# Recurrent chunk states of a hybrid encoder block: the scaling by the decay moves from VectorE to ScalarE

## The chip, the cores and the metric

The kernel runs on one core of one Trainium2 chip. The metric is device time in microseconds, the median of several runs. Engines are called as the profile calls them: PE is TensorE's matmuls, DVE is VectorE, ACT is ScalarE, POOL is GpSimd, SP is the engine that issues most DMAs.

## What is computed

One layer of an encoder on x of 1 x 1024 x 1024 in float32: a layer norm; one large projection `h @ w_in`; a dilated sliding-window attention; a bidirectional gated recurrence (HGRN2) of 8 heads with 128 keys and 128 values each; gates and output projections; two more layer norms around a SwiGLU feed-forward part. The change lies in the recurrence, which the reference computes by chunks of 64 tokens (cut):

```
def gla_chunkwise(q, k, v, logf):
    cum = jnp.cumsum(logf.reshape(b, h, n, c, kd), axis=3)
    q_dec = q * jnp.exp(cum)
    ...
    cum_last = cum[..., -1:, :]
    u = jnp.einsum('bhnck,bhncv->bhnkv', k * jnp.exp(cum_last - cum), v)
    decay = jnp.exp(cum_last[..., 0, :])

    def step(state, inp):
        d, uu = inp
        return d[..., None] * state + uu, state
    ...
    o_inter = jnp.einsum('bhnck,bhnkv->bhncv', q_dec, s_start)
```

It is done twice, forward and on the flipped sequence. The state of a chunk is a 128 x 128 matrix per head and direction.

## The kernel before

**The stream of projections.** The first part of the kernel (`phase1`, L1214) is a stream of projection products on PE. Each float32 matrix is split into a high part, cast by ACT (L212), and a low part, a subtraction on POOL (L220); a product is three matmuls (L268, L269, L270). The big products are formed from sums of blocks in the manner of Strassen and Winograd, so that sums of weights (L606 and neighbours) come before the matmuls and evacuations (L484, L509, L510, L633 and others, on DVE and ACT) come after them. Products use four PSUM banks, called pj.

**The side work.** Between the steps of that stream, a generator takes a step of the recurrence or of the attention: heads 0 and 1, a unit of attention, heads 2 and 3, a unit, heads 4 and 5, a unit, heads 6 and 7. This lies between 145 and 1010 us. All of it uses four more PSUM banks, called sd, that rotate (`ps_sd`). The program is written in this order, and the framework's scheduler, which simulates a timeline, moves instructions of each engine; each engine then takes its own queue strictly in order.

**One head** (`hgrn_side`, L1174). Chunks are taken as 8 blocks of 128 tokens, with gates scaled around the middle of each block, so that the decay of a whole block is the product of two factors: `dec[:, 0]` from the middle to the block's end and `dec[:, 1]` from its start to the middle.
- `hgrn_dir` (L1044), once per direction: gates and scans, reciprocals (L1079, L1082), the scaled queries `qd` (L1083, L1084; L1083 is also the last reader of the tile `fa`), and the decays, copied by POOL (L1088, L1089).
- `hgrn_keys` (L1091): PE transposes four blocks of keys into an sd bank (L1097), ACT copies them out to `hkT` (L1098); two banks per direction.
- `hgrn_states` (L1102): PE makes the seven chunk products (L1113) into two sd banks, four and three. DVE runs the chain E: L1122 for the first block, then for each of the other six L1124 (E times `dec[:, 1]` plus the product, read from PSUM) and L1125 (times `dec[:, 0]`). After each block ACT writes E times `dec[:, 1]` into the state tile S, called `hS` (L1116). A state is 13 operations of DVE and 7 of ACT; there are 16 states, 8 heads by 2 directions.
- S is a slot of 1024 columns: that of direction 0 is where `fa` was, that of direction 1 is where the second direction's `fb` was. The chain's tiles `hR` rotate among three.
- `hgrn_scores` (L1129), twice, each for four blocks and with two sd banks: L1138 to L1142. They need no state.
- `hgrn_out` (L1152): the scores times values plus `qd` times S, L1164.

The order within a head is: keys of direction 0, states 0, keys of direction 1, states 1, both halves of the scores, output. Since sd banks rotate, the scores' second pair of banks are those of a states step before it, and a bank can be written again only when its last reader is through.

Of the kernel before, what the change touches and what calls it, by code (L numbers as in the profile page):

```python
# [10 lines left out]
F32 = mybir.dt.float32  # L11
F32R = mybir.dt.float32r
I32 = mybir.dt.int32
AF = mybir.ActivationFunctionType
OP = mybir.AluOpType
# [57 lines left out]


CST_PAD = 32
SMT_PAD = 832
TABW = 128 * 5 + 64 + 256 + 384 + 256 + 192


class Block:  # L80
# [963 lines left out]
    def hgrn_dir(self, h, d, st):  # L1044

        nc = self.nc
        ga, gb, gna = (z[:, d, h:h + 1] for z in (self.ga, self.gb, self.gna))
        t3 = st[f"t{d}"].rearrange("p (c i) -> p c i", i=128)
        q3 = st["q"].rearrange("p (c i) -> p c i", i=128)

        A = st["fa"][:, HALF * d:HALF * d + HALF].rearrange("p (c i) -> p c i", i=64)
        B = self.slot(7 + d, "fb", (8, 66))
        if d == 0:
            nc.gpsimd.memset(A[:, :, 0:1], 0.0)
            nc.gpsimd.memset(B[:, :, 65:66], 0.0)
            nc.scalar.activation(A[:, :, 1:64], t3[:, :, 65:128], AF.Identity, bias=gb, scale=ga)
            nc.scalar.activation(B[:, :, 0:65], t3[:, :, 0:65], AF.Identity, bias=gb, scale=ga)
        else:
            nc.gpsimd.memset(A[:, :, 63:64], 0.0)
            nc.gpsimd.memset(B[:, :, 0:1], 0.0)  # L1060
            nc.scalar.activation(A[:, :, 0:63], t3[:, :, 0:63], AF.Identity, bias=gb, scale=ga)
            nc.scalar.activation(B[:, :, 1:66], t3[:, :, 63:128], AF.Identity, bias=gb, scale=ga)
        nc.gpsimd.tensor_scalar(t3, t3, gna, ga, op0=OP.mult, op1=OP.add)

        def scan(f, n, rev):
            f = f.rearrange("p c i -> p (c i)")
            f = f[:, ::-1] if rev else f
            nc.vector.tensor_tensor_scan(f, f, self.d1[n], 0.0, op0=OP.mult, op1=OP.add)

        scan(A, 64, d == 1)  # L1070
        scan(B, 66, d == 0)
        far = slice(64, 128) if d == 0 else slice(0, 64)
        near = slice(0, 64) if d == 0 else slice(64, 128)
        R = B[:, :, 1:65]
        qd = self.slot(2 + 2 * d, "qd", (8, 128))
        nc.gpsimd.tensor_mul(t3[:, :, near], t3[:, :, near], R)
        yield
        for c in (slice(0, 4), slice(4, 8)):
            nc.vector.reciprocal(qd[:, c, far], A[:, c])  # L1079
        nc.gpsimd.tensor_mul(t3[:, :, far], t3[:, :, far], qd[:, :, far])  # L1080
        for c in (slice(0, 4), slice(4, 8)):
            nc.vector.reciprocal(qd[:, c, near], R[:, c])  # L1082
        nc.vector.scalar_tensor_tensor(qd[:, :, far], q3[:, :, far], CQ, A, op0=OP.mult, op1=OP.mult)  # L1083
        nc.vector.scalar_tensor_tensor(qd[:, :, near], q3[:, :, near], CQ, qd[:, :, near], op0=OP.mult, op1=OP.mult)  # L1084
        st["qd", d], st["ki", d] = qd, t3

        dec = st["dec", d] = self.smt.tile([128, 2, 8], F32, name="dec", tag="dec", bufs=4)
        nc.gpsimd.tensor_copy(dec[:, 0, :], A[:, :, 63 if d == 0 else 0])  # L1088
        nc.gpsimd.tensor_copy(dec[:, 1, :], B[:, :, 0 if d == 0 else 65])  # L1089

    def hgrn_keys(self, st, d):  # L1091

        nc, out = self.nc, []
        for b in (0, 1) if d == 0 else (1, 0):
            pt, kT = self.ps_sd(), self.half3("hkT")
            for k in range(4):
                nc.tensor.transpose(pt[:, 128 * k:128 * (k + 1)], st["ki", d][:, 4 * b + k, :], self.ident)  # L1097
            nc.scalar.copy(kT, pt.rearrange("p (k c) -> p k c", k=4))  # L1098
            out.append(kT)
        return out  # L1100

    def hgrn_states(self, st, d, kT, vT):  # L1102

        nc, dec = self.nc, st["dec", d]
        S = self.slot(6 + d, "hS", (8, 128))
        cs = list(range(8)) if d == 0 else list(range(7, -1, -1))
        E = None
        for b in range(2):
            ps = self.ps_sd().rearrange("p (k c) -> p k c", k=4)
            part = cs[4 * b:4 * b + 4]  # L1110
            for jj, c in enumerate(part):
                if c != cs[-1]:
                    nc.tensor.matmul(ps[:, jj, :], kT[b][:, c % 4, :], vT[:, c, :], start=True, stop=True)  # L1113
            for jj, c in enumerate(part):
                if E is not None:
                    nc.scalar.activation(S[:, c, :], E, AF.Copy, scale=dec[:, 1, c:c + 1])  # L1116
                if c == cs[-1]:
                    continue

                En = self.sm.tile([128, 128], F32, name="hR", tag="hR", bufs=3)  # L1120
                if E is None:
                    nc.vector.tensor_scalar(En, ps[:, jj, :], dec[:, 0, c:c + 1], None, op0=OP.mult)  # L1122
                else:
                    nc.vector.scalar_tensor_tensor(En, E, dec[:, 1, c:c + 1], ps[:, jj, :], op0=OP.mult, op1=OP.add)  # L1124
                    nc.vector.tensor_scalar(En, En, dec[:, 0, c:c + 1], None, op0=OP.mult)  # L1125
                E = En
        return S

    def hgrn_scores(self, st, b):  # L1129
# [84 lines left out]
    def phase1(self):  # L1214
# [9 lines left out]
        self.smt = side.enter_context(self.pool("smt"))  # L1224
        self.pad(self.smt, SMT_PAD)
        self.cst1 = side.enter_context(self.pool("cst1"))
# [623 lines left out]
```

## Time and profile before

| | us |
|---|---|
| median of 3 runs | 2102.98 |
| lowest and highest | 2100.78 and 2104.03 |
| the profiled execution | 2102.44 |
| span of its profile | 2100.6 |
| busy in the span: POOL | 1093.8 |
| the largest group on POOL, L220 from `wa`, 272 times | 377.1 |
| the largest group on ACT, L212 from `wa`, 272 times | 167.6 |

The span is what the profile covers of the execution; the rest lies around it. Rows of a page or a view give the line of the kernel, the engine, the operation, output and inputs, and the shape. A number after `x` is a count. In a timeline a row begins with the start and the duration in us, and brackets hold the idle time before it and what ended it. In a group's row, after the bar, come busy us and the mean ns of one instruction, then the idle time before and what ended it. The granted clock is the share of TensorE's full rate that the throttle allowed in a stretch; its mean in this execution is 0.987. A busy PE at half the clock does half the work.

### The profile page before, as it was taken

The page shows a single profiled execution, that of the slowest core. Times are in us where ns is not written, and L with a number is a line of the kernel's source. Part 1 is how long each engine was busy: PE and PEld are TensorE (multiplying, and loading weights), DVE is VectorE, ACT ScalarE, POOL GpSimd, SP SyncE. Part 2 cuts the span into 40 slices and gives each one's busy share as a digit, 9 for nine tenths or more (in the row PEclk, how much of TensorE's full clock was granted, in tenths as well). Part 3 has the DMA queues.
Part 4 walks back from the last instruction along what each step waited for, and adds up shares of the span by engine and source line. Part 5 has one row for each costly group of instructions (what it writes and reads, how often), then busy time and mean ns, then how long its engine had stood idle before and what let it go on. Part 6 is the DMA issues. An engine that isn't in the chain of part 4 may idle for free.

```text
span 2100.6 us, 30922 instructions
## 1 busy us (share of the span) xinstructions
PE 2025.1 (96%) x10974; PEld 1675.0 (80%) x10974; DVE 1380.4 (66%) x2158; ACT 931.8 (44%) x1878; POOL 1093.8 (52%) x903
## 2 busy tenths in 40 slices
PE   6799999999999999999999899999999999999998
PEld 4588788888887888887888788888788888887876
DVE  7777645885468854788444722347867777767777
ACT  6544455444554436543365531144433333334542
POOL 6476654576446763565635854244666666630012
PEclk9899999999999999999999999999999999999999
DMA  4343442435333353343534764344434344347423
GB/s 146 111 145 111 152 136 94 143 131 161 125 132 113 118 169 109 111 131 121 163 106 157 267 213 150 100 141 135 157 124 147 131 148 133 121 158 288 160 91 125
DMA packets 274845, 297.95 MB, mean 142 GB/s; under 512 B 14018, under 2 KB 207363, under 8 KB 274691
## 3 DMA queue, kind: packets, MB, share of 16 engines
q1 hardware_dynamic: 268384, 274.78, 40.5%
q10 hardware_dynamic: 6306, 21.20, 2.6%
q8 instruction: 86, 1.41, 0.3%
q14 instruction: 69, 0.56, 0.1%
HBM read 201.29 MB, written 94.63 MB: 141 GB/s over the span
## 4 chain that ended last, share of the span: by engine, by line
PE 79%; DVE 9%; issue 5%; POOL 3%; DMA 3%; ACT 1%; SPq 0%; ACTq 0%; DVEq 0%; POOLq 0%
PE pj L268 17%; PE pj L270 17%; PE pj L269 17%; PE sd L269 6%; PE sd L268 6%; PE sd L270 6%; PE sd L1164 2%; POOL w_lo L220 2%; DVE qd L1079 1%; PE sd L920 1%; PE sd L969 1%; PE sd L996 1%; PE sd L1113 1%; DVE hR L1125 1%; PE sd L696 1%
## 5 line engine op out<-in xcount | busy, mean ns | idle before, releaser
L220 POOL TENSOR_TENSOR w_lo<-wa,w_hi 128x512 fp32r<-128x512 f32 x272 | 377.1, 1394 | 290.6 <-ACT w_hi L212 258.9
L212 ACT CAST w_hi<-wa 128x512 fp32r<-128x512 f32 x272 | 167.6, 619 | 249.9 <-PE pj L269 142.9
L220 POOL TENSOR_TENSOR w_lo<-wsum,w_hi 128x512 fp32r<-128x512 f32 x88 | 126.3, 1444 | 113.6 <-PE sd L270 57.5
L220 POOL TENSOR_TENSOR w_lo<-f_raw,w_hi 128x512 fp32r<-128x512 f32 x66 | 102.1, 1554 | 55.7 <-ACT w_hi L212 54.5
L208 POOL TENSOR_TENSOR mv<-mv,mhalf 128x1 f32<-128x1 f32 x16 | 10.8, 679 | 208.2 <-DVE mv L207 208.0
L212 ACT CAST w_hi<-wsum 128x512 fp32r<-128x512 f32 x88 | 54.7, 622 | 126.1 <-PE sd L269 117.7
L268 PE MATMUL pj<-xt1hi,w_hi 128*128 128x512 f32 x252 | 100.6, 399 | 4.9 <-ACT wkeep L633 2.7
L268 PE MATMUL pj<-xb22hi,w_hi 128*128 128x512 f32 x252 | 99.3, 394 | 0.0
L270 PE MATMUL pj<-xb22hi,w_lo 128*128 128x512 f32 x252 | 98.4, 391 | 0.8 <-POOL w_lo L220 0.8
L269 PE MATMUL pj<-xt1lo,w_hi 128*128 128x512 f32 x252 | 99.1, 393 | 0.0
L270 PE MATMUL pj<-xt1hi,w_lo 128*128 128x512 f32 x252 | 98.8, 393 | 0.0
L269 PE MATMUL pj<-xb22lo,w_hi 128*128 128x512 f32 x252 | 98.3, 390 | 0.0
L220 POOL TENSOR_TENSOR w_lo<-ws,w_hi 128x512 fp32r<-128x512 f32 x46 | 64.8, 1414 | 56.0 <-ACT w_hi L212 53.2
L212 ACT CAST gwsum<-a_raw 128x512 fp32r<-128x512 f32 (+1 forms) x78 | 47.7, 616 | 101.4 <-PE pj L269 46.3
L633 ACT COPY wkeep<-pj 128x512 f32<-128x512 f32 x136 | 79.3, 583 | 28.8 <-DVE evh L511 13.3
L268 PE MATMUL pj<-xt2hi,w_hi 128*128 128x512 f32 x192 | 78.6, 410 | 10.8 <-ACT xt2hi L212 10.8
L484 DVE TENSOR_TENSOR evh<-wkeep,pj 128x512 f32<-128x512 f32 x66 | 57.6, 880 | 44.3 <-PE pj L270 29.7
L606 POOL TENSOR_TENSOR wa<-wa,wa 128x512 f32<-128x512 f32 x46 | 69.4, 1517 | 31.2 <-DVE ws L605 28.5
L220 DVE TENSOR_TENSOR gwkeep<-a_raw,gwsum 128x512 fp32r<-128x512 f32 (+1 forms) x78 | 57.7, 739 | 41.9 <-ACT gwsum L212 39.0
L495 DVE TENSOR_TENSOR evh<-wkeep,pj 128x512 f32<-128x512 f32 x45 | 30.6, 683 | 78.7 <-PE pj L270 59.0
L268 PE MATMUL pj<-xb11hi,w_hi 128*128 128x512 f32 x192 | 77.3, 405 | 3.4 <-ACT xb11hi L212 2.3
L1116 ACT ACTIVATE hS<-hR,dec 128x128 f32<-128x128 f32 x112 | 44.4, 402 | 76.7 <-DVE hR L1125 46.9
(418 smaller groups left out, 6659.7 us busy)
## 6 DMA issues: line engine op xcount, KB each, us to landing
wa<-in_w_in_dram SPq DMA_DIRECT2D x184, 256.0 KB, 3.3
f_raw<-in_w_ffn_in_dram SPq DMA_DIRECT2D x44, 512.0 KB, 4.0
a_raw<-gd SPq DMA_DIRECT2D x30, 512.0 KB, 3.6
gd<-fc SPq DMA_DIRECT2D x44, 256.0 KB, 2.0
gd<-fs SPq DMA_DIRECT2D x33, 256.0 KB, 2.1
tg<-evh SPq DMA_DIRECT2D x32, 256.0 KB, 3.1
tg<-tg SPq DMA_DIRECT2D x16, 512.0 KB, 3.5
y<-ahs SPq DMA_DIRECT2D x16, 512.0 KB, 4.9
```

The source lines that it names most:

```text
L212: ins = nc.scalar.copy(hi, src) if eng_hi == "act" else nc.vector.tensor_copy(hi, src)
L220: ins = e.tensor_sub(lo, src, hi.bitcast(F32))
L268: nc.tensor.matmul(ps, whi, xhi, start=first, stop=False, **kw)
L269: nc.tensor.matmul(ps, whi, xlo, start=False, stop=False, **kw)
L270: self.product = nc.tensor.matmul(ps, wlo, xhi, start=False, stop=last, **kw).ins.name
L484: self.left(nc.vector.tensor_tensor(o, self.order_src(add, g, kind), s, OP.add))
L495: self.left(nc.vector.tensor_add(t, add, ps))
L606: nc.gpsimd.tensor_sub(a["a21"], a["a11"], a["a21"])
L633: nc.scalar.copy(t, ps)
L696: nc.tensor.transpose(ps[:, 128 * k:128 * (k + 1)], cols(4 * b + k), self.ident)
L1116: nc.scalar.activation(S[:, c, :], E, AF.Copy, scale=dec[:, 1, c:c + 1])
L1164: nc.tensor.matmul(po[:, jj, :], l, r, start=(n == 0), stop=(n == len(terms) - 1))
```

## The change

The decay tile gets a third row, the product of the two factors, one POOL multiply of 128 x 8 per state. In `hgrn_states`, ACT first takes all products of a bank out of PSUM, scaled by `dec[:, 0]`, into the S cells of the blocks that follow. DVE's chain then begins with the first S cell as it stands, and each further step is one operation, E times `dec[:, 2]` plus the S cell, both read from SBUF. After each step ACT writes E times `dec[:, 1]` over the S cell; the first cell is scaled in place, once the second step has been made from it. A state is then 6 operations of DVE and 14 of ACT. `SMT_PAD` keeps the tiles behind the decays at their places. A line of before beyond L1090 moves; the scores' L1141 is L1142 afterwards, and the key copy's L1098 is L1099.

```diff
@@ -73,7 +73,7 @@
 
 
 CST_PAD = 32
-SMT_PAD = 832
+SMT_PAD = 704
 TABW = 128 * 5 + 64 + 256 + 384 + 256 + 192
 
 
@@ -1084,9 +1084,10 @@
         nc.vector.scalar_tensor_tensor(qd[:, :, near], q3[:, :, near], CQ, qd[:, :, near], op0=OP.mult, op1=OP.mult)
         st["qd", d], st["ki", d] = qd, t3
 
-        dec = st["dec", d] = self.smt.tile([128, 2, 8], F32, name="dec", tag="dec", bufs=4)
+        dec = st["dec", d] = self.smt.tile([128, 3, 8], F32, name="dec", tag="dec", bufs=4)
         nc.gpsimd.tensor_copy(dec[:, 0, :], A[:, :, 63 if d == 0 else 0])
         nc.gpsimd.tensor_copy(dec[:, 1, :], B[:, :, 0 if d == 0 else 65])
+        nc.gpsimd.tensor_mul(dec[:, 2, :], dec[:, 0, :], dec[:, 1, :])
 
     def hgrn_keys(self, st, d):
 
@@ -1101,29 +1102,29 @@
 
     def hgrn_states(self, st, d, kT, vT):
 
+
         nc, dec = self.nc, st["dec", d]
         S = self.slot(6 + d, "hS", (8, 128))
         cs = list(range(8)) if d == 0 else list(range(7, -1, -1))
         E = None
         for b in range(2):
             ps = self.ps_sd().rearrange("p (k c) -> p k c", k=4)
-            part = cs[4 * b:4 * b + 4]
-            for jj, c in enumerate(part):
-                if c != cs[-1]:
-                    nc.tensor.matmul(ps[:, jj, :], kT[b][:, c % 4, :], vT[:, c, :], start=True, stop=True)
-            for jj, c in enumerate(part):
-                if E is not None:
-                    nc.scalar.activation(S[:, c, :], E, AF.Copy, scale=dec[:, 1, c:c + 1])
-                if c == cs[-1]:
-                    continue
-
-                En = self.sm.tile([128, 128], F32, name="hR", tag="hR", bufs=3)
+            part = [(jj, c, cs[4 * b + jj + 1]) for jj, c in enumerate(cs[4 * b:4 * b + 4]) if c != cs[-1]]
+            for jj, c, _ in part:
+                nc.tensor.matmul(ps[:, jj, :], kT[b][:, c % 4, :], vT[:, c, :], start=True, stop=True)
+            for jj, c, after in part:
+                nc.scalar.activation(S[:, after, :], ps[:, jj, :], AF.Copy, scale=dec[:, 0, c:c + 1])
+            for jj, c, after in part:
                 if E is None:
-                    nc.vector.tensor_scalar(En, ps[:, jj, :], dec[:, 0, c:c + 1], None, op0=OP.mult)
+                    E = S[:, after, :]
                 else:
-                    nc.vector.scalar_tensor_tensor(En, E, dec[:, 1, c:c + 1], ps[:, jj, :], op0=OP.mult, op1=OP.add)
-                    nc.vector.tensor_scalar(En, En, dec[:, 0, c:c + 1], None, op0=OP.mult)
-                E = En
+                    En = self.sm.tile([128, 128], F32, name="hR", tag="hR", bufs=3)
+                    nc.vector.scalar_tensor_tensor(En, E, dec[:, 2, c:c + 1], S[:, after, :], op0=OP.mult, op1=OP.add)
+                    E = En
+                if after != cs[1]:
+                    nc.scalar.activation(S[:, after, :], E, AF.Copy, scale=dec[:, 1, after:after + 1])
+                    if after == cs[2]:
+                        nc.scalar.activation(S[:, cs[1], :], S[:, cs[1], :], AF.Copy, scale=dec[:, 1, cs[1]:cs[1] + 1])
         return S
 
     def hgrn_scores(self, st, b):
```

## The prediction

> **What bounds the kernel now.** I read, in this order: the page's busy shares, stretches of 50 us, TensorE's waits in the part that has recurrent states (145 to 1010 us), and then the timeline around each of those waits.
>
> ```profile
> PE 2025.1 (96%) x10974; PEld 1675.0 (80%) x10974; DVE 1380.4 (66%) x2158; ACT 931.8 (44%) x1878; POOL 1093.8 (52%) x903
> ```
> ```profile
> 250.00:300.00 50.00, 50.00 (x323) 41.54 (x322) 22.73 (x84) 21.91 (x61) 28.59 (x27) 1.00 0.52 165
> 650.00:700.00 50.00, 45.08 (x294) 38.31 (x293) 36.72 (x57) 22.51 (x46) 27.46 (x29) 0.93 0.35 117
> ```
> The columns of the second view are length, then busy time of PE, PEld, DVE, ACT and POOL, clock, DMA share and GB/s. TensorE (PE) is busy 96% of the span, and all of 250 to 300, where no states are computed. In 650 to 700, with the states of head 4, it loses 5 us and its clock falls to 0.93. So DVE's and ACT's time counts only where TensorE waits for it:
>
> ```profile
> PE sd L1141 <- DVE hR L1124: 6.5, 3, 3.5
> PE sd L1113 <- ACT hkT L1098: 4.7, 4, 1.6
> PE pj L268 <- ACT wkeep L633: 2.7, 1, 2.7
> PE pj L268 <- DVE evh L484: 2.6, 3, 1.6
> PE pj L268 <- DVE wkeep L509: 1.1, 1, 1.1
> PE pj L270 <- POOL w_lo L220: 0.6, 2, 0.5
> ```
> (Who waits, for whom, us in all, times, longest.) Two rows touch the states. In the first, the second half of the scores (L1141) wants PSUM banks which the DVE chain of the other direction (L1124) has not read out yet. In the second, the chunk products (L1113) want turned keys that ACT has not copied yet (L1098). Their places:
>
> ```profile
> 230.35 1.83 PE L1113 MATMUL sd<-hv,hkT 128*128 128x128 f32 x14 [1.59 <-ACT hkT L1098]
> 240.39 0.27 PE L1141 MATMUL sd<-qd,t 128*64 128x64 f32 x1 [2.07 <-DVE hR L1124]
> 420.60 0.27 PE L1141 MATMUL sd<-qd,t 128*64 128x64 f32 x1 [1.02 <-DVE hR L1124]
> 658.78 2.10 PE L1113 MATMUL sd<-hv,hkT 128*128 128x128 f32 x14 [1.46 <-ACT hkT L1098]
> 673.12 0.37 PE L1141 MATMUL sd<-qd,t 128*64 128x64 f32 x1 [3.46 <-DVE hR L1124]
> 980.33 1.16 PE L1113 MATMUL sd<-hv,hkT 128*128 128x128 f32 x8 [0.91 <-ACT hkT L1098]
> 982.20 1.47 PE L1113 MATMUL sd<-hv,hkT 128*128 128x128 f32 x6 [0.71 <-ACT hkT L1098]
> ```
> The brackets hold TensorE's idle time and what ended it. The heads are 1 (two rows), 2, 4 (two), and 7 (two). After two of the bank waits the clock falls as well:
>
> ```profile
> 240.40:246.00 5.60, 5.60 (x46) 4.69 (x47) 2.75 (x6) 2.44 (x6) 3.80 (x5) 0.70 0.48 143
> 673.10:680.00 6.90, 6.88 (x47) 5.86 (x48) 5.25 (x8) 1.72 (x4) 3.46 (x4) 0.60 0.57 184
> ```
> Clock 0.70 over 5.60 us loses 0.30 x 5.60 = 1.7 us; 0.60 over 6.90 us loses 2.8 us. So the bank waits cost 2.07 + 1.02 + 3.46 = 6.55 us themselves and 4.5 us behind them.
>
> **The change part by part.** *DVE.* The rows of the chain (busy us, mean ns; the last is the tile's view, min/median/max):
>
> ```profile
> L1125 DVE TENSOR_SCALAR hR<-hR,dec 128x128 f32<-128x128 f32 x96 | 46.3, 483 | 2.9
> L1124 DVE SCALAR_TENSOR_TENSOR hR<-hR,dec,sd 128x128 f32<-128x128 f32 x96 | 33.3, 346 | 8.3
> L1122 DVE TENSOR_SCALAR hR<-sd,dec 128x128 f32<-128x128 f32 x16 | 5.3, 331 | 6.6 <-PE sd L1113 6.4
> L1125 DVE TENSOR_SCALAR hR<-hR,dec x96: 272/287/1344, 150.8 to 993.7; 128x128 f32<-128x128 f32 x96
> ```
> Removed: 96 x 0.483 + 16 x 0.331 = 51.7 us. The 96 operations of L1124 stay, but read both operands from SBUF. No row shows that form, so I bound it: below by the fastest SBUF-only operation, 0.272; above by today's 0.346 plus the time by which L1125's mean exceeds its median, 0.483 - 0.287 = 0.196, which gives 0.542. I take 0.45, nearer to L1125's mean, since that is the SBUF-only neighbour. DVE then saves 51.7 - 96 x 0.10 = 42 us (33 to 59). Almost none of it counts by itself: DVE is busy 66%.
>
> *ACT.* 112 scalings become 224 (per state 7 + 7).
>
> ```profile
> L1116 ACT ACTIVATE hS<-hR,dec 128x128 f32<-128x128 f32 x112 | 44.4, 402 | 76.7 <-DVE hR L1125 46.9
> L719 ACT COPY pf<-sd 128x256 f32<-128x256 f32 x16 | 5.2, 376 | 2.7 <-PE sd L825 2.6
> L310 ACT ACTIVATE tsv<-sd,vc 128x128 f32<-128x128 f32 x38 | 15.3, 457 | 13.0 <-DVE tsv L312 5.3 <-PE sd L300 5.1 <-DVE xt2lo L220 1.5
> ```
> A scaling out of PSUM is not there; the plain copy out of PSUM takes 0.376 for twice the columns, and a two-operand activation out of PSUM 0.457. I take today's 0.40, as the nearest in form. The next ACT operation starts 0.31 us after a scaling starts (below: 657.85, then 658.16), so seven in a row hold ACT for 7 x 0.31 = 2.2 us, and 112 for 35 us. What covers this is the lead of the casts that ACT makes for the projections. The tightest I found in a state's stretch is this one:
>
> ```profile
> 659.79 0.62 ACT L212 CAST w_hi<-wa 128x512 fp32r<-128x512 f32 x1
> 660.48 1.29 POOL L220 TENSOR_TENSOR w_lo<-wa,w_hi 128x512 fp32r<-128x512 f32 x1 [1.58 <-ACT w_hi L212]
> 665.29 0.39 PE L270 MATMUL pj<-xb21hi,w_lo 128*128 128x512 f32 x1
> ```
> The low part is ready at 661.77 and is first used at 665.29: 3.5 us of lead, more than 2.2. And of L220 TensorE waits 0.6 us in all. So I cost the extra ACT time at nothing on this path; without that cover it is up to 2.2 us per state.
>
> *POOL, PSUM, queues.* Sixteen 128x8 multiplies, by the 222 ns of the copies beside them, are 3.6 us of POOL:
>
> ```profile
> L1089 POOL COPY dec<-fb 128x8 f32<-128x8 f32 x16 | 3.5, 222 | 0.0
> ```
> POOL is busy 52%, and the product is ready before keys are turned: nothing. Matmuls stay (10974 records); seven short groups slide by a few places. No DMA is added; three issues swap places. The padding and the third row of `dec` do no work.
>
> *The bank waits.* A bank is now free when ACT has made its last scaling, not when DVE's chain has passed it. At head 4 the chain of direction 1 reads its last product here:
>
> ```profile
> 667.26 0.35 DVE L1124 SCALAR_TENSOR_TENSOR hR<-hR,dec,sd 128x128 f32<-128x128 f32 x1
> 672.72 0.34 DVE L1124 SCALAR_TENSOR_TENSOR hR<-hR,dec,sd 128x128 f32<-128x128 f32 x1
> ```
> That is 672.72 + 0.34 = 673.06, and TensorE goes on at 673.12. It came there at 673.12 - 3.46 = 669.66. The seven products are done at 658.78 + 2.10 = 660.9; seven scalings need 2.2 us, and with two casts and an evacuation among them (0.62, 0.62 and 0.6 us) they end near 665, some 4 us early. At head 2 the products of the state in question end here:
>
> ```profile
> L1113 PE MATMUL sd<-hv,hkT x9: 271/275/293, 404.8 to 409.3; 128*128 128x128 f32 x9
> ```
> That is 409.3 + 0.28 = 409.6, with the scalings 411.8, against a wish at 420.60 - 1.02 = 419.6. Head 1 is the tight one: products at 230.35 + 1.83 and the 1.0 of the next part, 233.2, with the scalings 235.4, with 2.4 us of casts, evacuations and the other direction's scalings among them (my estimate, from 0.6 us each) 237.8, against a wish at 240.39 - 2.07 = 238.3. All three waits go: **-6.55 us**. What is late next at L1141 is nothing that I can see. Head 4's low clock goes with its wait: **-2.8 us**. Head 1's I keep (0 us), since its key wait, below, grows to about the 2.07 that sufficed there.
>
> Here a rule of the Trainium skill stands against a row. "TensorE: Matmul & The Clock Gate", section "Why this matters for your kernels", warns only of idle gaps above about 3 us, and Part 1 there gives an idle window of about 3.4 us. The row differs: 0.70 follows a wait of 2.07. By the rule head 1's low clock would go too, and the sum would be 1.7 us lower; the measurement decides.
>
> *The key copies.* ACT takes its queue in order. Where the keys of direction 1 are copied behind the scalings of direction 0, seven stand now ahead of them where one or two stood:
>
> ```profile
> 229.43 0.40 ACT L1116 ACTIVATE hS<-hR,dec 128x128 f32<-128x128 f32 x1 [5.70 <-DVE hR L1125]
> 229.74 1.05 ACT L1098 COPY hkT<-sd 128x512 f32<-128x512 f32 x2
> 657.85 0.40 ACT L1116 ACTIVATE hS<-hR,dec 128x128 f32<-128x128 f32 x1 [1.62 <-DVE hR L1122]
> 658.16 0.57 ACT L1098 COPY hkT<-sd 128x512 f32<-128x512 f32 x1
> 729.38 0.57 ACT L1098 COPY hkT<-sd 128x512 f32<-128x512 f32 x1
> 730.00 1.83 PE L1113 MATMUL sd<-hv,hkT 128*128 128x128 f32 x14
> 981.58 0.56 ACT L1098 COPY hkT<-sd 128x512 f32<-128x512 f32 x1
> ```
> But ACT idled there for DVE (5.70 and 1.62 us in the brackets), and part of the seven fits into that idle time. Following the changed order: head 1's keys come 1.0 us later (three chain steps more stand ahead of them), head 4's 0.3, head 5's 0.45 (its products followed 0.05 us behind the copy, 729.95 to 730.00), head 7's 0.8 (three scalings of the second bank). Each can be 0.3 us less or up to 2.2 us more. Heads 0, 2, 3 and 6 have lead for it. **+2.55 us**. The first DVE operation of a chain now waits for ACT's second scaling; queued behind it on DVE are evacuations of the projections, which today wait behind 13 chain operations rather than 6, so I cost that wait at nothing; if ACT comes late it is again the 2.2 us.
>
> *Sum.* -6.55 - 2.8 + 2.55 = -6.8 us. The profiled execution took 2102.44 us (span 2100.6, 1.84 around it), 0.54 below the median of 2102.98. I take the difference from the median: **2096.2 us**. About 0.2% (4.2 us) is what a measurement of this kernel can tell from no change: faster is below 2098.8, slower above 2107.2.
>
> **The rivals.**
>
> *A. The chain is blocked in SBUF.* The mean of 483 against a median of 287 on L1125 says that SBUF-only operations of DVE lose 0.2 us on average to something, up to 1.06 us at once. If the new operation loses more than I allow, each state's six steps take 6 x 0.2 = 1.2 us longer, and ACT's scalings behind them hold the keys at heads 1, 4, 5 and 7 by about that: 4 x 1.2 - 6.8 = -2.0 us, 2101.0. For it: the maximum of 1344 ns. Against: the banks no longer hang on the chain. The Trainium skill, "SBUF — State Buffer", section "SBUF: two separate sides", says that a DVE operation with two SBUF inputs and a GpSimd operation that reads SBUF exclude each other for the whole instruction, as one in a 2-port mode does; L1125's spread agrees with that, and no row here shows the two-input form.
>
> *B. The change doesn't do what it says.* The scalings come as late as the chain did, because they stand behind casts and evacuations in ACT's queue; the banks are freed no earlier and the keys are still late: 2102.98 + 2.55 = 2105.5. Against: head 4 has 4 us to spare.
>
> *C. The seven scalings hold the keys.* Slower: at each of heads 1, 4, 5 and 7 the whole 2.2 us lands ahead of the key copy, and the longer wait brings a low clock like that of head 1, 1.7 us: 4 x 3.9 = 15.6, less the 9.35 gained, is +6.3: 2109.3. It decides from the point where the key waits and what follows them grow by more than 9.35 us, 2.3 per head. For it: in-order queue, and all four copies stand behind the block. Against: ACT's idle time ahead of the scalings (5.70 us at head 1).
>
> **How the numbers follow.** Forecast 0.50 (own range 2092 to 2099, by 0.3 us less or 0.7 more at each of four keys and by the clock), the same with head 1's clock free 0.05 (2094.5), A 0.17, B 0.09, C 0.19. Faster: 0.50 + 0.05, less 0.02 of the forecast's edge, 0.53; within 0.2%: 0.17 + 0.09 + 0.02 = 0.28; slower: 0.19. The range reaches from 2090 (no key later and head 1's clock free: 2102.98 - 9.35 - 1.7 = 2091.9, less the 1.6 us by which the runs before spread to a side) to 2108.5, which takes in A, B, and C where a little less than the whole 2.2 us lands.
>
> **What would show it.** The waits for DVE at L1141 (one line lower afterwards) should be gone and no wait for ACT's scalings stand in their place; the stretch at 673 should be back near clock 1.00; waits for the key copies should grow from 4.7 to about 7 us, at 230 and 980 above all. DVE's busy time should be near 1338 us, ACT's near 970 (112 x 0.40 = 45 us by durations at most, 35 by starts), and the new operation near 0.45 us. The forecast is wrong if TensorE waits for casts (L220, L268) inside the states' stretches, if key waits exceed 9 us, or if stretches without states change length.

## The result, and the profile after

The changed kernel took 2091.23 us (median of 5, 2086.52 to 2093.86), the kernel before 2101.64 us in the same comparison (median of 5, 2099.73 to 2104.03). The ratio is 0.9955 with a 95% interval of 0.9943 to 0.9967: 9.5 us faster, between 6.9 and 12.0. A second comparison on another occasion gave 2091.24 us and 0.9958 (0.9945 to 0.9970). The forecast was 6.8 us faster, 2096.2 us. The 2091.23 us lie inside its wide range, 2090 to 2108.5, and just below the narrow one, 2092 to 2099; the kernel before was itself 1.3 us faster in this comparison than in the runs that the forecast was counted from. The profiled execution took 2093.86 us, its span is 2092.0.

The page of the changed kernel, busy time by engine:

```profile
PE 2018.3 (96%) x10974; PEld 1670.2 (80%) x10974; DVE 1349.8 (65%) x2046; ACT 956.5 (46%) x1990; POOL 1095.3 (52%) x919
```

DVE's busy time fell by 30.6 us and ACT's rose by 24.7, both less than forecast (42, and 35 to 45). The same stretches of 50 us as before, and then two stretches around the old places of low clock (length, then PE, PEld, DVE, ACT, POOL, clock, DMA, GB/s):

```profile
250.00:300.00 50.00, 50.00 (x323) 41.53 (x322) 22.74 (x84) 21.92 (x60) 28.59 (x27) 1.00 0.51 161
650.00:700.00 50.00, 46.20 (x304) 38.61 (x303) 38.76 (x45) 26.51 (x62) 31.95 (x34) 1.00 0.38 127
```
```profile
240.00:246.00 6.00, 6.00 (x94) 5.14 (x93) 3.42 (x6) 2.96 (x9) 3.72 (x5) 1.00 0.39 121
673.10:680.00 6.90, 6.07 (x50) 5.43 (x48) 1.83 (x4) 4.14 (x10) 5.35 (x6) 1.00 0.57 192
```

The stretch without states is what it was. At 240 and at 673 the clock is full. TensorE's waits between 145 and 1010 us, and the places of the longest ones:

```profile
PE sd L1114 <- ACT hkT L1099: 5.7, 4, 2.6
PE pj L268 <- DVE evh L484: 4.7, 4, 2.4
PE pj L268 <- ACT wkeep L633: 1.4, 1, 1.4
PE pj L268 <- DVE wkeep L509: 1.3, 1, 1.3
PE sd L1098 <- POOL t L1076: 1.0, 1, 1.0
PE sd L1165 <- POOL ham L1148: 0.8, 1, 0.8
```
```profile
232.83 0.42 PE L1114 MATMUL sd<-hv,hkT 128*128 128x128 f32 x1 [2.61 <-ACT hkT L1099]
657.27 0.49 PE L1114 MATMUL sd<-hv,hkT 128*128 128x128 f32 x2 [0.61 <-ACT hkT L1099]
699.46 0.47 PE L268 MATMUL pj<-xt4hi,w_hi 128*128 128x512 f32 x1 [2.37 <-DVE evh L484]
975.10 0.38 PE L1114 MATMUL sd<-hv,hkT 128*128 128x128 f32 x1 [1.86 <-ACT hkT L1099]
```

The scores' wait for the chain (6.5 us, L1141, now L1142) has no row any more. The wait for key copies went from 4.7 to 5.7. New is 2.37 at 699.46, where the kernel before had 0.44. Its cause stands on DVE (two rows of the changed kernel, then the same evacuation and product in the kernel before):

```profile
695.08 3.35 DVE L1079 RECIPROCAL qd<-fa 128x256 f32<-128x256 f32 x2
698.35 1.92 DVE L484 TENSOR_TENSOR evh<-wkeep,pj 128x512 f32<-128x512 f32 x2
```
```profile
703.74 1.93 DVE L484 TENSOR_TENSOR evh<-wkeep,pj 128x512 f32<-128x512 f32 x2
704.86 0.47 PE L268 MATMUL pj<-xt4hi,w_hi 128*128 128x512 f32 x1 [0.44 <-DVE evh L484]
```

The evacuation that TensorE needs stands in DVE's queue behind two reciprocals of the next head. It did so before as well: there it starts at 703.74, 5.4 us later. But TensorE came 7.3 us later to this place (704.86 - 0.44 = 704.42, against 699.46 - 2.37 = 697.09). TensorE gained more than DVE's queue did, and waits for the rest. So of the 3.46 us taken away at 673, about 1.9 come back here.

**Where the 9 us came from.** In 145 to 1010 us TensorE idles 865 less its busy time. The row of before, then of the changed kernel:

```profile
145.00:1010.00 865.00, 845.51 (x5494) 707.31 (x5494) 577.88 (x1045) 414.39 (x937) 501.09 (x460) 0.99 0.40 129
```
```profile
145.00:1010.00 865.00, 849.34 (x5541) 711.95 (x5541) 549.97 (x938) 442.05 (x1055) 508.69 (x479) 1.00 0.41 132
```

That is 19.5 us of idling against 15.7, 3.8 less. And counted in the trace's clock records of that part, there were 5 stretches of 3.41 us at half clock before and 2 after. Each costs 3.41 / 2 = 1.7 us, so 5.1 less. Together 8.9, against 8.6 between the two spans. In this pair of executions more than half of the gain is clock. Over many executions it is less: on one chip the mean granted clock was 0.9890 in 22 runs of the kernel before and 0.9903 in 11 of the change, which by 2100 x 0.0013 is 2.7 us of the 8.8 between their mean times (an estimate).

### The profile page after: what moved, and what is told of

Its sections match the earlier page's. It is cut to its first block, busy times and chain, and to the rows that moved or that the text cites. A ratio compares the mean times of both kernels' runs of the same rounds, so it can differ in the third digit from the quotient of the medians.

```text
span 2092.0 us, 30925 instructions
## 1 busy us (share of the span) xinstructions
PE 2018.3 (96%) x10974; PEld 1670.2 (80%) x10974; DVE 1349.8 (65%) x2046; ACT 956.5 (46%) x1990; POOL 1095.3 (52%) x919
## 4 chain that ended last, share of the span: by engine, by line
PE 80%; DVE 9%; issue 4%; DMA 3%; POOL 3%; ACT 1%; SPq 0%; ACTq 0%; DVEq 0%; POOLq 0%
PE pj L268 17%; PE pj L269 17%; PE pj L270 17%; PE sd L268 6%; PE sd L269 6%; PE sd L270 6%; PE sd L1165 2%; POOL w_lo L220 2%; PE sd L1114 1%; DVE qd L1079 1%; PE sd L920 1%; PE sd L969 1%; PE sd L996 1%; DVE qd L1082 1%; DMA att<-ol 1%
## 5 line engine op out<-in xcount | busy, mean ns | idle before, releaser
L220 POOL TENSOR_TENSOR w_lo<-wa,w_hi 128x512 fp32r<-128x512 f32 x272 | 376.0, 1390 | 282.9 <-ACT w_hi L212 261.4
L212 ACT CAST w_hi<-wa 128x512 fp32r<-128x512 f32 x272 | 168.5, 622 | 264.1 <-PE pj L269 156.1
L220 POOL TENSOR_TENSOR w_lo<-wsum,w_hi 128x512 fp32r<-128x512 f32 x88 | 126.6, 1447 | 113.0 <-PE sd L270 60.7
L220 POOL TENSOR_TENSOR w_lo<-f_raw,w_hi 128x512 fp32r<-128x512 f32 x66 | 102.3, 1557 | 55.8 <-ACT w_hi L212 54.6
L212 ACT CAST w_hi<-wsum 128x512 fp32r<-128x512 f32 x88 | 54.7, 621 | 126.4 <-PE sd L269 118.5
L212 ACT CAST gwsum<-a_raw 128x512 fp32r<-128x512 f32 (+1 forms) x78 | 47.7, 615 | 100.3 <-PE pj L269 46.0
L633 ACT COPY wkeep<-pj 128x512 f32<-128x512 f32 x136 | 79.7, 586 | 26.3 <-DVE evh L511 12.3
L220 POOL TENSOR_TENSOR w_lo<-ws,w_hi 128x512 fp32r<-128x512 f32 x46 | 64.5, 1408 | 50.7 <-ACT w_hi L212 50.5
L484 DVE TENSOR_TENSOR evh<-wkeep,pj 128x512 f32<-128x512 f32 x66 | 57.7, 879 | 49.7 <-PE pj L270 36.3
L220 DVE TENSOR_TENSOR gwkeep<-a_raw,gwsum 128x512 fp32r<-128x512 f32 (+1 forms) x78 | 57.7, 739 | 40.9 <-ACT gwsum L212 38.1
L495 DVE TENSOR_TENSOR evh<-wkeep,pj 128x512 f32<-128x512 f32 x45 | 30.6, 683 | 79.3 <-PE pj L270 56.2
L268 PE MATMUL pj<-xt4hi,w_hi 128*128 128x512 f32 x192 | 77.0, 401 | 2.5 <-DVE evh L484 2.4
```

The source lines that it names most:

```text
L212: ins = nc.scalar.copy(hi, src) if eng_hi == "act" else nc.vector.tensor_copy(hi, src)
L220: ins = e.tensor_sub(lo, src, hi.bitcast(F32))
L268: nc.tensor.matmul(ps, whi, xhi, start=first, stop=False, **kw)
L484: self.left(nc.vector.tensor_tensor(o, self.order_src(add, g, kind), s, OP.add))
L495: self.left(nc.vector.tensor_add(t, add, ps))
L633: nc.scalar.copy(t, ps)
```

## The experiments

All were compared with runs of the kernel before on their own chip; the medians of those lie between 2100.18 and 2101.64 us, and the differences below are worked out from the ratios where nothing else is said. This table is for orientation; idle is 865 less TensorE's busy time in 145 to 1010 us, half counts the stretches of 3.41 us at half clock there. Both are of one profiled execution of each kernel.

| kernel | median us | ratio to before (95%) | idle us | half |
|---|---|---|---|---|
| before | 2101.64 | | 19.5 | 5 |
| the change | 2091.23 | 0.9955 (0.9943 to 0.9967) | 15.7 | 2 |
| direction 1 new | 2095.89 | 0.9981 (0.9972 to 0.9989) | 18.4 | 4 |
| direction 0 new | 2095.45 | 0.9977 (0.9966 to 0.9989) | 19.1 | 2 |
| one step per chunk from PSUM | 2088.47 | 0.9945 (0.9933 to 0.9956) | 17.3 | 0 |
| ACT copies, chain of two steps | 2107.61 | 1.0031 (1.0020 to 1.0042) | 25.8 | 3 |
| the change, keys 1 copied by DVE | 2095.65 | 0.9982 (0.9971 to 0.9993) | 19.3 | 1 |
| the change, PSUM scalings twice | 2101.08 | 1.0001 (0.9991 to 1.0011) | 22.0 | 3 |
| the change, chain twice | 2105.76 | 1.0027 (1.0016 to 1.0037) | 25.4 | 4 |
| one step from PSUM, keys first | 2082.21 | 0.9917 (0.9901 to 0.9932) | 10.9 | 0 |
| the change, keys first | 2089.50 | 0.9942 (0.9929 to 0.9956) | 12.1 | 2 |
| before, keys first | 2103.69 | 1.0014 (1.0004 to 1.0023) | 21.0 | 6 |
| one step, keys first, ACT twice | 2096.33 | 0.9985 (0.9974 to 0.9996) | 19.4 | 2 |
| the change again | 2091.24 | 0.9958 (0.9945 to 0.9970) | 14.4 | 1 |

The theory was that of the prediction, that banks freed early by ACT are the gain. Its rivals were DVE's load, and the clock.

**Half of the change: direction 1.** The old function is kept beside the new one:

```diff
+    def hgrn_states(self, st, d, kT, vT):
+        return (self.hgrn_states_new if d == 1 else self.hgrn_states_old)(st, d, kT, vT)
```

> States of direction 1 in the new form, those of direction 0 in the old one. Theory (banks): the gain comes from PSUM banks that the scores want, and these are held by the chain of direction 1; so the three waits of L1141 for the chain (6.5 us) go, the key copies, which stand behind direction 0's ACT work, stay near 4.7 us, and the kernel is 8 to 10 us faster than before, as much as the whole change or a little more. Rival (load): the gain comes from a lighter DVE, spread over all 16 states; then half of the change gives half the gain, 4 to 5 us. Rival (clock): the waits matter little and the gain is that three stretches of 3.4 us at half clock happened to be missing; then TensorE's idle time in 145 to 1010 us falls by under 2 us, and the time lies anywhere within 5 us of before.

Measured: 4.0 us faster (ratio 0.9981), the rival's number. The scores' waits are gone, as the theory had it, but the key copies wait longer:

```profile
PE sd L1144 <- ACT hkT L1099: 6.9, 5, 2.4
PE pj L268 <- DVE evh L484: 4.7, 4, 2.4
```

Most of the removed 6.5 us came back, 2.2 at the keys, 2.1 at L484 and the rest at smaller waits, and idling fell by 1.1 us only. Freed banks alone are not the gain. But the rival of the clock had forecast as much: idling down by under 2 us, and a time within 5 us of before.

**The other half: direction 0.**

```diff
+    def hgrn_states(self, st, d, kT, vT):
+        return (self.hgrn_states_new if d == 0 else self.hgrn_states_old)(st, d, kT, vT)
```

> States of direction 0 in the new form, those of direction 1 in the old one. Theory (banks): the scores' waits for the DVE chain stay at some 6 us, and the key copies of direction 1 stand behind seven scalings; the time is that of before or up to 2.5 us more. Rival (load): 4 to 5 us faster. Rival (clock): anywhere within 5 us of before, with no relation to the waits.

Measured: 4.8 us faster (0.9977). This is the rival's number again, and the theory falls:

```profile
PE sd L1117 <- ACT hkT L1099: 5.6, 4, 2.3
PE sd L1172 <- DVE hR L1128: 3.3, 2, 3.1
```

Of the three waits for the chain of direction 1 one is left, of 3.1 us, and 0.2 us of another, although that chain is the old one. Both chains go through one queue on DVE, so when the first is short, the second ends earlier: at head 1 its last product is read at 239.22 us where it was 239.99. There this is less than half of what the wait lost; TensorE also came 1.1 us later.

The two halves do not tell load from clock. Idling fell by 1.1 and 0.4 us, and the mean granted clock of their 11 and 12 runs is 0.9896 for 0.9884 in the 26 runs beside them, some 2.5 us of the 4.0 and 4.8 (an estimate). Low clock itself follows idle windows, as the last section shows, so it is no cause apart from the waits; where it falls is partly chance.

**The chain in one step without ACT.** The chain carries the state before its last decay, and the decays of two neighbours are multiplied on POOL, so that DVE's single step can read the product in PSUM, and ACT has its 7 scalings of before.

```diff
-        nc.gpsimd.tensor_mul(dec[:, 2, :], dec[:, 0, :], dec[:, 1, :])
+        to, fr = (slice(1, 8), slice(0, 7)) if d == 0 else (slice(0, 7), slice(1, 8))
+        nc.gpsimd.tensor_mul(dec[:, 2, to], dec[:, 0, fr], dec[:, 1, to])
...
-                nc.scalar.activation(S[:, after, :], ps[:, jj, :], AF.Copy, scale=dec[:, 0, c:c + 1])
...
+                if E is None:
+                    nc.vector.tensor_copy(En, ps[:, jj, :])
+                else:
+                    nc.vector.scalar_tensor_tensor(En, E, dec[:, 2, c:c + 1], ps[:, jj, :], op0=OP.mult, op1=OP.add)
+                E = En
+                nc.scalar.activation(S[:, after, :], E, AF.Copy, scale=dec[:, 2, after:after + 1])
```

> Both directions: the chain carries the state before its last decay, so that one DVE operation per chunk, from PSUM, and one ACT scaling, by the product of two neighbouring decays, are enough: 7 + 7 operations per state, none of them added on ACT. Theory (banks): the chain frees its last bank after 7 x 0.35 = 2.4 us of DVE, nearly as early as ACT's seven scalings, so the scores' waits fall below 1 us; ACT's queue is no longer than before, so the key copies do not come later than before: 9 to 12 us faster than before, at least as fast as the change. Rival (load): DVE saves 46 us or more, so 10 us or more as well. Rival (the scaling out of PSUM by ACT is what is needed): banks are held by DVE, behind its evacuations of the projections, the waits of L1141 stay at 3 us or more and the gain is under 5 us.

Measured: 11.6 us faster (0.9945), and no wait of the scores for the chain is left. ACT's scalings out of PSUM are not what is needed; the short chain is. One expectation failed: the wait for key copies rose from 4.7 to 6.2 us with no operation added on ACT.

**ACT out of PSUM, chain as long as before.**

```diff
-                nc.scalar.activation(S[:, after, :], ps[:, jj, :], AF.Copy, scale=dec[:, 0, c:c + 1])
+                nc.scalar.copy(S[:, after, :], ps[:, jj, :])
...
+                    nc.vector.scalar_tensor_tensor(En, E, dec[:, 1, c:c + 1], S[:, after, :], op0=OP.mult, op1=OP.add)
+                    nc.vector.tensor_scalar(En, En, dec[:, 0, c:c + 1], None, op0=OP.mult)
```

> Both directions: ACT copies the products out of PSUM unscaled, and DVE's chain has its 13 operations as before, now from SBUF. Theory (banks): banks are freed by ACT as in the change, so the scores' waits for the chain go and most of the gain is there, 5 to 9 us faster than before, less what the longer chain holds up behind it. Rival (load): DVE is as busy as before or more (1380 us), so no gain, or slower.

Measured: 6.5 us slower than before (1.0031), the rival's side. The banks are free early, and nothing is won. The first row is TensorE's, the second POOL's:

```profile
PE sd L1162 <- POOL ham L1145: 10.2, 4, 5.0
POOL ham L1144 <- DVE amy L1142: 17.4, 12, 2.3
```

`ham` are the masked scores. DVE reads the scores out of PSUM (the `copy_predicated` of `hgrn_scores`), behind the chain in its queue, then POOL adds and the output's matmuls wait. The wait has only moved from the banks to the scores' read-out. The chain has as many operations as before, but from SBUF they are slower: they take 99.4 us of DVE where they took 84.9, so this run is not the early release alone.

**The change with the chain made twice.**

```diff
                     nc.vector.scalar_tensor_tensor(En, E, dec[:, 2, c:c + 1], S[:, after, :], op0=OP.mult, op1=OP.add)
+                    nc.vector.scalar_tensor_tensor(En, E, dec[:, 2, c:c + 1], S[:, after, :], op0=OP.mult, op1=OP.add)
```

> The changed kernel with each DVE operation of the chain made twice (12 instead of 6 per state; about 48 us more DVE time); the banks are still freed by ACT. Theory (DVE's time): what the change saves is DVE's time in the states' stretches, so most of the gain is lost: 2099 to 2107, and TensorE waits for what stands on DVE behind the chain (the scores' read-out, evacuations). Rival (banks): the wait that counts is the one for the banks, and ACT frees them as early as in the change: at most 2 us more than the change, 2091 to 2093.

Measured: 2105.76 us, 1.0027 against the change's 0.9955, so some 15 us dearer, as DVE's time would have it. The chain now takes 94.6 us of DVE for 49.6 in the change. The wait is at the same place as in the run above:

```profile
PE sd L1166 <- POOL ham L1149: 10.0, 6, 4.0
```

That is a third of a us for each us of chain. With the chain's 84.9 us of before, the early release would by this rate be some 2 us slower than before (an estimate: -9.5 + 35.3 / 3): alone it gains nothing.

**The change with ACT's scalings out of PSUM made twice.**

```diff
                 nc.scalar.activation(S[:, after, :], ps[:, jj, :], AF.Copy, scale=dec[:, 0, c:c + 1])
+                nc.scalar.activation(S[:, after, :], ps[:, jj, :], AF.Copy, scale=dec[:, 0, c:c + 1])
```

> The changed kernel with each scaling out of PSUM made twice, seven more ACT operations per state (about 1.9 us of ACT each state, by the seven that took 1.91 us in the changed kernel's profile). Theory (DVE's time): ACT has room in these stretches, so at most 3 us more than the change, 2089 to 2094. Rival (ACT's block holds the keys): the key copies come 1.9 us later in four heads or more, with low clock behind some of them, 8 us or more: 2099 or more.

Measured: 2101.08 us, 1.0001, 9.7 us more than the change. So ACT has no room there, and the theory of DVE's time alone is wrong too. But the rival's mechanism is not seen either:

```profile
PE pj L268 <- DVE evh L484: 6.4, 4, 3.4
PE sd L1140 <- ACT hS L1117: 4.9, 2, 2.5
PE sd L1114 <- ACT hkT L1099: 2.8, 4, 1.7
PE sd L1143 <- ACT hS L1117: 1.9, 1, 1.9
```

The keys wait less (2.8 for 5.7). What comes back is the scores' wait for banks, 4.9 + 1.9 = 6.8 us, now for ACT, which reads them out too late. In the change ACT is thus in time by less than the 1.9 us that were added.

**The key copies of direction 1 by DVE.**

```diff
-            nc.scalar.copy(kT, pt.rearrange("p (k c) -> p k c", k=4))
+            (nc.vector.tensor_copy if d else nc.scalar.copy)(kT, pt.rearrange("p (k c) -> p k c", k=4))
```

> The changed kernel with the key copies of direction 1 made by DVE instead of ACT. If ACT's block of scalings is what makes those copies late, TensorE's wait for them (5.7 us) falls under 2 us and the kernel is 3 to 5 us faster than the change, near 2087. If it is work on DVE that is late (the chain starts behind evacuations there), the copies wait in DVE's queue, the wait stays at 4 us or grows, and the time is that of the change or up to 4 us more.

Measured: 2095.65 us (0.9982), 4.4 us more than the change by the medians and 5.7 by the ratios. The products then wait 4.6 us for copies on DVE, and 2.6 and 1.3 us for ACT:

```profile
PE sd L1114 <- DVE hkT L1099: 4.6, 3, 2.4
PE sd L1114 <- ACT w_hi L212: 2.6, 1, 2.6
PE sd L1114 <- ACT hS L1125: 1.3, 1, 1.3
```

Both queues are late by as much, so moving the copy from one to the other gains nothing.

**Keys first.** Then the order was changed instead, the keys of direction 1 ahead of the states of direction 0, in three kernels:

```diff
         k0 = self.hgrn_keys(st, 0)
         yield 3
-        S = {0: self.hgrn_states(st, 0, k0, vT)}
         k1 = self.hgrn_keys(st, 1)
+        S = {0: self.hgrn_states(st, 0, k0, vT)}
```

With the one-step chain from PSUM:

> The kernel with one DVE step per chunk from PSUM and 7 scalings on ACT per state, and the keys of direction 1 turned before the states of direction 0. Theory (the keys of direction 1 are late because their copies stand in ACT's queue behind scalings that wait for the chain): TensorE's wait for key copies, 6.2 us there, falls under 2 us, and the time from 2088.5 to about 2084. Rival (something else is late by as much: the evacuations, the DMA that frees their buffers): the wait moves to another place, and the time stays within 2 us of 2088.5.

Measured: 2082.21 us, 0.9917 (0.9901 to 0.9932), 17 us faster than before and the fastest of all. These are all waits of TensorE above 0.5 us in 145 to 1010:

```profile
PE pj L268 <- DVE evh L484: 4.7, 4, 2.4
PE pj L268 <- ACT wkeep L633: 2.3, 1, 2.3
PE pj L268 <- DVE wkeep L509: 1.3, 1, 1.3
PE sd L1137 <- DVE hR L1120: 0.9, 1, 0.9
PE sd L1160 <- POOL ham L1143: 0.9, 1, 0.9
```

With the change:

> The changed kernel with the keys of direction 1 turned before the states of direction 0. Theory (with the short chain the keys are the next wait, and it does not come back elsewhere): TensorE's wait for key copies, 5.7 us, falls under 1 us and the time to about 2085. Rival (the wait comes back at another place, as after other edits): within 2 us of the change.

Measured: 2089.50 us (0.9942), 1.7 us below the change's median, with intervals that overlap. The wait for key copies is gone, but 3.2 us at `ham` have come for it; that is nearer to the rival.

With the kernel before:

> The kernel before with the keys of direction 1 turned before the states of direction 0. Theory (with the long chain DVE sets the pace of these stretches): the wait for key copies, 4.7 us, goes, but TensorE then comes earlier to the banks which the chain holds, the scores' wait for the chain grows from 6.5 us to 9 us or more, and the time stays within 3 us of before. Rival (the two waits are independent): 5 to 8 us faster than before, as the same edit gave with the one-step chain.

Measured: 2103.69 us, 1.0014 (1.0004 to 1.0023), about 3 us slower. As expected of the long chain, the wait for the keys went and the waits for the chain took its place:

```profile
PE sd L1141 <- DVE hR L1124: 10.8, 6, 3.8
PE sd L1138 <- DVE hR L1124: 1.8, 2, 0.9
```

4.7 + 6.5 = 11.2 us of waits became 12.6. With the long chain, DVE sets the pace. The clock fell too: in the mean 0.986 over its 11 runs, for 0.989 in the 17 beside them.

**ACT's price with the short chain.** The fastest kernel with each of its ACT scalings made twice, 14 per state as in the change:

```diff
                 nc.scalar.activation(S[:, after, :], E, AF.Copy, scale=dec[:, 2, after:after + 1])
+                nc.scalar.activation(S[:, after, :], E, AF.Copy, scale=dec[:, 2, after:after + 1])
```

> The kernel with one DVE step per chunk from PSUM and keys first (2082 us), with each ACT scaling made twice: 14 per state, as many as in the change. It asks why the change with keys first stands at 2089.5 and not at 2082. If ACT's seven operations more per state are the reason: 2087 to 2091. If it is DVE's operation, which takes 0.35 us from PSUM and SBUF and 0.5 us from SBUF alone: ACT's operations cost little, 2081 to 2085.

Measured: 2096.33 us (0.9985), 14 us more: ACT's seven more operations per state cost more than either number expected. The chain's group and the scores' wait:

```profile
L1120 DVE SCALAR_TENSOR_TENSOR hR<-hR,dec,sd 128x128 f32<-128x128 f32 x96 | 33.3, 347 | 25.1 <-ACT hS L1123 22.1
```
```profile
PE sd L1138 <- DVE hR L1120: 7.5, 4, 2.3
```

DVE stood idle 22.1 us in the chain because ACT had not yet read `hR`, of which there are three. So an ACT that is behind holds up the chain on DVE, the chain holds the banks, and the scores wait for them. Without the doubling the same group idles 9.4 us in all, 1.0 of it for ACT.

**The change again.**

> The change itself once more, on the same chip as the run beside it, for its profile and time: 2088 to 2094. If low clock follows a wait by where the wait lies in a grid of 3.41 us, and that grid does not start with the kernel, the waits are those of the first profile within 0.3 us each, and the half-clock stretches may stand at other waits of 1.9 to 3 us; if low clock follows each wait above some length, they stand at the same waits, 232.8 and 699.5.

Measured: 2091.24 us. The two long waits stand at the same instructions as in the first profile, with 2.42 and 2.36 us for 2.61 and 2.37:

```profile
231.36 0.87 PE L1114 MATMUL sd<-hv,hkT 128*128 128x128 f32 x3 [2.42 <-ACT hkT L1099]
697.20 0.47 PE L268 MATMUL pj<-xt4hi,w_hi 128*128 128x512 f32 x1 [2.36 <-DVE evh L484]
```
```profile
231.54:234.95 3.41, 3.41 (x16) 3.31 (x17) 0.53 (x2) 3.41 (x10) 1.96 (x2) 0.50 0.21 77
697.00:704.00 7.00, 6.80 (x39) 5.88 (x39) 5.84 (x9) 1.69 (x3) 2.94 (x3) 1.00 0.59 212
```

Half clock follows the first wait, and not the second, though the second is as long as its fellow in the first profile, behind which it did follow. So it is not the length of a wait alone. The last section says what it is.

## Why the prediction was right, and where not

**Banks.** All three waits for the chain went, as forecast. That ACT's early release is the reason is only half of it. With the release and a chain of 13 operations the kernel is 6.5 us slower than before (and some 2 us slower by the estimate above, if those operations cost no more than before); with the short chain and no such release it is 11.6 us faster. The step "What is late next at L1141 is nothing that I can see" holds only since the chain is short as well. Otherwise the scores' read-out stands late behind the chain on DVE, and TensorE waits 10 us for it.

**DVE's saving.** "Almost none of it counts by itself: DVE is busy 66%" is the step that failed. 66% is a mean over the span. In the stretches with states, DVE's queue is what TensorE waits for next, and 45 us more of chain cost 15 us of time. The saving was also over-estimated. The new operation took more than the 0.45 us that I chose:

```profile
L1122 DVE SCALAR_TENSOR_TENSOR hR<-hR,dec,hS 128x128 f32<-128x128 f32 x80 | 40.0, 500 | 13.0 <-ACT hS L1125 7.4
L1122 DVE SCALAR_TENSOR_TENSOR hR<-hS,dec 128x128 f32<-128x128 f32 x16 | 9.6, 601 | 17.1 <-ACT hS L1116 16.2 <-POOL w_lo L220 0.9
```

(40.0 + 9.6) / 96 = 0.517 us. The chain's own rows fell from 84.9 to 49.6 us, by 35.3, within the 33 to 59. DVE's busy time as a whole, in which operations that overlap count once, fell by 30.6; its other operations took 2.7 us longer in sum.

**ACT's cost at nothing** failed too. I looked for the cover at the casts, and there it held: no wait for L212 or L220 shows in the changed kernel between 145 and 1010 us. But I cost the chain's wait for ACT at nothing as well, and the last parts of the two rows above hold it, 16.2 us ahead of the first step and 7.4 ahead of the others. That is idle time of DVE. What it costs in time is less clear: against the one-step chain without added ACT operations the change is 2 us slower, with intervals that overlap, and with keys first 5 us, or 7 by the medians, with intervals that just touch. DVE's form differs as well between these two.

**Key copies.** +1.0 us in place of +2.55. Head 1 came as worked out (2.61 - 1.59 = 1.02 later), head 7 by 0.24 instead of 0.8, head 5 not at all, head 2 by 0.6 that I had given lead for, and head 4 was 0.85 better. At head 4 ACT's seven came as one block, in 1.91 us:

```profile
654.83 1.91 ACT L1116 ACTIVATE hS<-sd,dec 128x128 f32<-128x128 f32 x7
656.58 0.64 ACT L1099 COPY hkT<-sd 128x512 f32<-128x512 f32 x1
```

Before, the copy stood behind one scaling that waited 1.62 us for the chain. The block waits for nobody. That is, at head 4, why rival C did not come: taking the chain out of what ACT waits for made up for the six operations more. C's price was real, since the same block made twice costs 9.7 us, but it is paid at the banks and not at the keys.

**Clock.** I counted 2.8 us at head 4, and measured 3.4 there (two stretches), and three other changes that I had not foreseen: the stretches behind 896 and 982 us are gone (-1.7 each), and one at 700 is new (+1.7); that of 240 is now at 233. The sum is -5.1, so in this pair of profiles the term was mis-sized by 2.3 us. Part of that is chance: the second profile of the change has one such stretch, not two, and over the 22 and 11 runs above the clock's part is 2.7 us, about what was counted for head 4.

**Not foreseen** were the waits that came back, 2.1 us at L484 and 1.6 at L1098 and L1165, and 1.7 us that went at L633, L509 and L220 together. With the banks' 6.55 and the keys' 1.0 this gives 3.6 us less idling by the rows, 3.8 by the busy time, where the forecast had 6.55 - 2.55 = 4.0. So in this pair of profiles the idling came out right in sum, by luck, from parts that were partly wrong, and the 2.3 us of clock are nearly the whole difference between 6.8 and 9.5. Over the runs it is the other way round: with 2.7 us of clock, some 6 us are left for the rest, where the forecast had 4.0. The second profile of the change idles 14.4 us, 5.1 less than before.

**Rivals.** A's mechanism is there (0.517 us, up to 1.43 us at once), at about a third of its price, 0.07 us a step above what I took in place of 0.2. B fell with the waits at L1141.

The Trainium skill, "SBUF — State Buffer", section "SBUF: two separate sides", was cited for A. This case now shows it. From PSUM and SBUF the step takes 333 to 350 ns (before); from SBUF alone (the change) the mean is 500 and the longest 1426 ns. Of the change's 96 steps the 63 during which POOL ran nothing took 337 to 354 ns, and the 33 that overlapped an operation of POOL took 836 in the mean. In the one-step chain from PSUM 54 of 96 steps overlapped one, and none took more than 350 ns. The ranges, before and in the change:

```profile
L1124 DVE SCALAR_TENSOR_TENSOR hR<-hR,dec,sd x96: 333/348/350, 150.4 to 992.4; 128x128 f32<-128x128 f32 x96
```

```profile
L1122 DVE SCALAR_TENSOR_TENSOR hR<-hR,dec,hS x80: 337/352/1426, 152.3 to 984.9; 128x128 f32<-128x128 f32 x80
```

**What stays open:** how much of the difference between the change and the one-step chain is ACT's operations and how much DVE's slower form. The doubled ACT operations show that the first alone can cost that much. The doubled ones all hang on the chain, though, while the change's scalings out of PSUM wait only for TensorE, so this is not the change's own price. The second was not tried by itself.

## What to carry to other kernels

An engine that is 66% busy over the span can still be the next thing that everything waits for in a stretch: read the queue of that stretch, and ask of each wait that goes what stands behind it in the same queue. Halving the number of dependent operations by algebra, here by carrying the state before its last decay, gained 11.6 us without moving an operation; moving the read-out to another engine gained nothing without it. The removal of one wait was worth little until the others with the same cause were gone: keys first cost 3 us with the long chain and brought 6 with the one-step chain from PSUM.

## What the runs showed of the hardware

**Low clock comes from a fixed grid.** In each trace the half-clock stretches start at multiples of 3.41 us from one another. Where these multiples lie differs between executions. Over the 14 profiles of this case I cut TensorE's time from 120 to 2040 us into these windows and took its idle time in each. Of 49 windows at full clock with 2.0 us or more of idling, all 49 were followed by one at half clock; of some thirty with 1.6 to 2.0, 11; of more than 7700 below 1.6, none. Windows that were themselves at half clock needed less: the 15 with 0.7 us or more were followed by another, the 58 with 0.6 or less by none. Before, at 238.31, and the change, at 697.25, each with its follower:

```profile
238.31:241.73 3.42, 1.35 (x36) 1.27 (x35) 3.01 (x9) 2.11 (x5) 0.83 (x1) 1.00 0.00 0
241.73:245.14 3.41, 3.41 (x9) 2.73 (x9) 1.42 (x4) 1.38 (x4) 2.17 (x4) 0.50 0.62 187
```
```profile
697.25:700.66 3.41, 1.20 (x5) 1.05 (x6) 3.41 (x4) 0.31 (x1) 2.75 (x3) 1.00 0.40 129
700.66:704.07 3.41, 3.41 (x9) 2.63 (x8) 3.41 (x6) 0.55 (x2) 0.00 (x0) 0.50 0.48 178
```

The idle times are 3.42 - 1.35 = 2.07 and 3.41 - 1.20 = 2.21 us. The same wait of the one-step chain, 2.40 us long, fell over the edge of two windows, with 0.85 us in the one and 1.55 in the next, and the clock stayed full:

```profile
694.27:697.68 3.41, 2.56 (x12) 1.79 (x10) 3.41 (x4) 0.94 (x2) 3.41 (x4) 1.00 0.27 77
697.68:701.10 3.42, 1.87 (x8) 1.60 (x9) 3.42 (x5) 0.00 (x0) 2.09 (x2) 1.00 0.53 176
```

So a wait of 2 to 3.4 us costs 1.7 us more or not, by where the grid lies in that execution (the longest without low clock behind it was 3.38 us, 1.9 in one window and 1.5 in the next), and several short waits can add up to it, as at 980 and 982 us in the kernel before. The Trainium skill, "TensorE: Matmul & The Clock Gate", Part 1, has the free-running window of about 3.4 us, and the traces agree; its limits, an idle window there and a gap above about 3 us in the section "Why this matters for your kernels", are not what they show, which is 2.0 us within one window.
